# A decoder step on one core: sample rows requested in other places, keys scaled for the state, transposes of two heads in one bank

## The chip, the cores and the metric

The kernel runs on one core of a Trainium2 chip. A core has five engines that each work through a list of their own, in order: TensorE (PE, matmuls and transposes; PEld is its weight load), VectorE (DVE), ScalarE (ACT), GpSimd (POOL) and SyncE (SP, which here only requests transfers; ScalarE requests some too). An instruction waits for semaphores of the others. The metric is the device time of one execution in microseconds.

## The reference

One layer of a decoder, for a prompt of 512 tokens and 8 samples of one token, D = 1024, all in float32:

```python
h = x * (1 + scale) + shift                       # adaLN: silu(c) @ w_ada, six parts
aq, ak, av, mq, mk, mv, mo, mi, mf = split(h @ w_in)
att = moba(aq, ak, av)                            # 8 heads x 64, softmax over blocks of 256 keys
  # samples: 4 pages of 128 keys each from cache_k, cache_v by page_table
C, n, m, hm = mlstm(mq, mk * 128**-0.5, mv, ig, lf)   # 4 heads x 128
  # C_new = g_inter * C + sum_j g_in[j] * v[j] k[j]^T
  # n_new = g_inter * n + sum_j g_in[j] * k[j]
mem = layernorm(hm) * g * sigmoid(mo)
x = layernorm(ALPHA * x + (1 + g1) * ([att, mem] @ w_out))
f = (silu(h2 @ w_gate) * (h2 @ w_up)) @ w_down    # h2: adaLN of x, width 2816
y = layernorm(ALPHA * x + (1 + g2) * f)
```

Outputs are y, the new keys and values, and the states C, n and m, for the prompt and for each sample.

## The kernel before

Each weight block of 128 x 1024 is loaded as float32 (`raw`) and split into two fp32r parts: `whi`, cast by ScalarE (L231), and `wlo` = raw - whi, by VectorE (L232). The activations are split likewise (`hT_hi`, `hT_lo`), and each product is three matmuls (hi x hi, hi x lo, lo x hi), the main matmuls (L391, L644).

The order of all work is written by a small scheduler at build time. A main stream goes through the blocks of w_in, w_out, w_gate, w_up and w_down. After some six main matmuls of 512 columns, or twelve of 256, it calls `tick` (L242): one step of every lane that is due, one weight split, and as many block loads as there are free raw buffers. A lane is a generator for a side job: a query tile of attention, an mLSTM head, a sample's state, the adaLN blocks (`ps_ada`, `ps_s`: rounds of small matmuls over a block). `yield n` in a lane puts its next part n ticks later. A lane that finds no free buffer or PSUM bank asks again in the next tick. So a `yield` moves instructions in the lists of all engines, against the main matmuls and against other lanes. There are eight PSUM banks, 22 large units, 13 halves, 6 rows and 4 squares. Each transfer takes the next of eight semaphores, and a request waits for the transfer that had that semaphore before.

The places that the change touches, in the order of time:

- Start: `cols` (conditioning columns, L285) is requested by ScalarE. `ps_warm` (L330) runs 12 dummy matmuls. `first_h` (L467) transposes the adaLN rows of a chunk (`ps_adat`), makes adaT, hT_hi (ScalarE) and hT_lo (VectorE), and for chunk 0 the first weight split.
- `att_unit(pair, qt)` (L795): for query tile qt and two heads, scores, softmax, then for each head transposes of the probabilities into a bank `ps_pt` and copies into `PT`; one bank a head.
- `sample_attention` (L1229): scores of all samples (`SC`) are transposed into `ps_ss`; own-token scores come from q8 and k8 (`qk`) through `own` and `ps_so`; the exponent `Pm` is read from ps_ss and ps_so; Pm is transposed (`ps_sp`), and `ps_pv` multiplies it with V pages, which `fetch` requests four at a time from SP, with a page number read from a table for each.
- `sample_bc(g)` (L1373): requests rows of k and q for four samples, broadcast over 32 partitions, by ScalarE, eight requests (`kq`). `sample_state(b)` (L1382): a sample's C is loaded, scaled by the forget gate on ScalarE, then on VectorE four state updates (L1393) and four dots (L1396).
- `mlstm_state` (L1155): the prompt's final C and n. Keys are transposed (`ps_mk`), copied (`mk`); values are multiplied by the input gate (`gv`, L1171); `ps_C` sums over tokens. `n_prompt_rows` (L1141) multiplies keys with the gate column.
- `out_fin` (L1699) of the samples: transposes `ps_xs` of the normalised rows.

## Time and profile before

| | |
|---|---|
| median of 3 runs | 795.07 us (792.77 to 795.56) |
| profiled execution | 797.14 us, span 795.4 us |
| mean granted clock of PE | 0.976 |
| PE busy | 756.5 us (95%) |
| PEld, DVE, ACT, POOL busy | 624.6, 408.7, 278.3, 136.7 us |
| chain that ended last | PE 81%, DVE 11%, issue 2%, DMA 2%, ACT 2%, POOL 1% |
| moved | 123.11 MB, mean 155 GB/s |

Times are microseconds from the start of the span. A row of the timeline gives the start, the time that the row's instructions took together (matmuls overlap, so the difference of two starts is what one takes), the engine and the line, and in brackets how long the engine had been idle and what released it. "SPq" and "ACTq" rows are requests of transfers; their time is the time that the engine's list spent on them.

### The profile page before, as it was taken

How to read it: one execution, taken by the hardware profiler on the slowest of the kernel's cores; microseconds unless marked ns; L12 is line 12 of the kernel's file. 1: busy time of each engine (PE TensorE's matmuls, PEld its weight loads, DVE VectorE, ACT ScalarE, POOL GpSimd, SP SyncE). 2: the span in 40 equal slices, each digit the busy share in tenths (PEclk: the TensorE clock that was granted, in tenths of full speed). 3: DMA queues.
4: the chain of work that ended last, by engine and by line, in shares of the span. 5: the costliest groups of instructions: out<-in, count | busy, mean ns of one | idle time of the engine just before them, and what ended most of it. 6: DMA issues, size and time to landing. Idle time of an engine off the chain costs nothing.

```text
span 795.4 us, 14683 instructions
## 1 busy us (share of the span) xinstructions
PE 756.5 (95%) x5790; PEld 624.6 (79%) x5790; DVE 408.7 (51%) x860; ACT 278.3 (35%) x556; POOL 136.7 (17%) x162
## 2 busy tenths in 40 slices
...
GB/s 344 361 215 165 271 209 192 213 203 143 177 206 261 332 207 202 276 71 213 133 137 89 124 109 133 83 103 107 80 80 80 99 87 102 85 80 106 1 42 67
DMA packets 105906, 123.11 MB, mean 155 GB/s; under 512 B 8220, under 2 KB 65696, under 8 KB 105836
## 3 DMA queue, kind: packets, MB, share of 16 engines
...
q10 hardware_dynamic: 8120, 9.23, 3.4%
...
## 4 chain that ended last, share of the span: by engine, by line
PE 81%; DVE 11%; issue 2%; DMA 2%; ACT 2%; POOL 1%; SPq 0%; POOLq 0%; ACTq 0%; DVEq 0%
PE acc L644 35%; PE acc L391 29%; PE ps_ada L405 2%; DVE wlo L232 2%; PE ps_dn L413 1%; PE accl L391 1%; PE ps_num L1061 1%; PE ps_pv L1307 1%; PE ps_sc L802 1%; PE ps_ada L459 1%; PE ps_o L855 1%; PE ps_pt L832 1%; PE ps_ms L1038 1%; DVE st L808 1%; DVE rtmp L1601 1%
## 5 line engine op out<-in xcount | busy, mean ns | idle before, releaser
L232 DVE TENSOR_TENSOR wlo<-raw,whi 128x1024 fp32r<-128x1024 f32 x104 | 138.0, 1334 | 124.5 <-ACT whi L231 117.2
L231 ACT CAST whi<-raw 128x1024 fp32r<-128x1024 f32 x104 | 108.0, 1049 | 154.1 <-PE acc L391 68.7
L644 PE MATMUL acc<-h_hi,whi 128*128 128x256 f32 (+1 forms) x640 | 129.2, 283 | 0.0
L644 PE MATMUL acc<-h_lo,whi 128*128 128x256 f32 (+1 forms) x640 | 128.3, 282 | 0.0
L644 PE MATMUL acc<-h_hi,wlo 128*128 128x256 f32 (+1 forms) x640 | 128.2, 282 | 0.0
L644 PEld LDWEIGHTS acc<-h_hi,whi 128*128 128x128 f32 x640 | 98.9, 188 | 2.6 <-issue 2.5
L644 PEld LDWEIGHTS acc<-h_lo,whi 128*128 128x128 f32 x640 | 99.3, 188 | 0.0
L644 PEld LDWEIGHTS acc<-h_hi,wlo 128*128 128x128 f32 x640 | 98.9, 188 | 0.0
L1216 POOL TENSOR_TENSOR kpage<-kpage,qb 128x512 f32<-128x512 f32 x32 | 42.5, 1352 | 81.2 <-DMA kpage<-in_cache_k_dram 80.8
L391 PE MATMUL acc<-whi,hT_hi 128*128 128x512 f32 x96 | 44.2, 460 | 2.1 <-DVE mv L1007 2.1
L1750 DVE TENSOR_TENSOR vf<-acc,vf 128x256 f32<-128x256 f32 x20 | 8.5, 424 | 72.1 <-PE acc L644 72.1
L391 PE MATMUL acc<-whi,f_hi 128*128 128x512 f32 x112 | 45.4, 405 | 0.0
L391 PE MATMUL acc<-whi,f_lo 128*128 128x512 f32 x112 | 44.2, 395 | 0.0
L391 PE MATMUL acc<-wlo,f_hi 128*128 128x512 f32 x112 | 44.2, 395 | 0.0
L391 PE MATMUL acc<-whi,hT_lo 128*128 128x512 f32 x96 | 39.7, 414 | 0.0
L391 PE MATMUL acc<-wlo,hT_hi 128*128 128x512 f32 x96 | 39.2, 409 | 0.0
L644 PE MATMUL acc<-hT_hi,whi 128*128 128x256 f32 (+1 forms) x160 | 35.9, 304 | 2.9 <-DVE mixA_lo L866 1.5
L1756 POOL COPY fsT<-vf 128x8 f32<-128x8 f32 x20 | 4.8, 239 | 192.5 <-DVE vf L1751 192.5
L397 ACT CAST f_hi<-vf 128x512 fp32r<-128x512 f32 (+1 forms) x24 | 14.0, 585 | 67.9 <-DVE vf L1751 61.9
L1602 POOL TENSOR_TENSOR x<-x,rtmp 128x512 f32<-128x512 f32 x16 | 26.0, 1642 | 65.2 <-DVE rtmp L1601 64.8
L644 PEld LDWEIGHTS acc<-hT_hi,whi 128*128 128x128 f32 x160 | 24.7, 188 | 13.2 <-issue 9.1
L644 PE MATMUL acc<-hT_hi,wlo 128*128 128x256 f32 (+1 forms) x160 | 32.1, 282 | 0.0
...
## 6 DMA issues: line engine op xcount, KB each, us to landing
...
```

Of the source, the lines that this page charges most:

```text
L231: ACOPY(out=t.hi_t, in_=t.raw)
L232: TT(out=t.lo_t, in0=t.raw, in1=t.hi_t, op=ALU.subtract)
L391: mm(ps, lhsT=a, rhs=b, start=start and i == 0, stop=stop and i == n - 1)
L397: ACOPY(out=dst_hi, in_=v)
L405: mm(ps[32 * c:32 * c + 32, 0:P], lhsT=lhs[:, k0 + kk, :], rhs=raw3[:, kk, ts(c, P)], start=start and kk == 0, stop=stop and kk == nk - 1, ...
L413: mm(ps[32 * c:32 * c + 32, 0:256], lhsT=lhs[:, k0 + kk, :], rhs=raw3[:, kk, ts(n, 256)], start=start, stop=stop, tile_position=(0, 32 * c))
L459: mm(ps[32 * c:32 * c + 32, 0:w], lhsT=siluT[:, k, :], rhs=rhs, start=k == 0, stop=k == 7, tile_position=(0, 32 * c))
L644: mm(accs[d, hf][:, 0:hi - lo], lhsT=w, rhs=two(xx, k)[:, lo:hi], start=k == 0 and i == 0, stop=k == 7 and i == 2)
L802: mm(bs[e][:, 0:n], lhsT=two(qT, pair)[eh, ts(qt, P)], rhs=two(kT, pair)[eh, 0:n], start=True, stop=True, tile_position=(64 * e, 0))
L1216: PT_(out=ks[i - 4], in0=ks[i - 4], in1=qb, op=ALU.mult)
L1602: (PT_ if pool_add else TT)(out=dst, in0=dst, in1=tmp, op=ALU.add)
L1750: TT(out=v[:, 0:HALF], in0=a[:, 0:HALF], in1=v[:, 0:HALF], op=ALU.mult)
```

## The change

`cols` is requested by SP. The warm-up has 10 dummies in place of 12; one dummy stands before the first ps_adat and five behind it, and for chunk 0 hT_lo is made ahead of the second half of the split. In att_unit both heads of a pair share a bank for qt 0 and 1, 256 columns each, and both are copied after the second; for qt 2 and 3 the second head comes a tick later. In sample_attention q8, k8 and v8 are requested ahead of the V pages, ps_so comes one tick later, ps_sp two later, ps_pv two ticks behind it, and the memset of its bank is replaced by a first matmul that writes 32 rows of each quadrant. kq is requested two at a time, a tick apart. A sample's dots come a tick after its updates. In mlstm_state the keys are multiplied by the input gate as they leave PSUM (two heads by ScalarE, two by VectorE); values go into ps_C as they are, and the n rows are summed with a column of ones. Two more `yield`s are longer by one (adaLN, ps_xs).

```diff
@@ -40,3 +40,3 @@
 N_HALVES = 13
-N_WARM = 12
+N_WARM = 10
 FF_GROUPS = ((0, 6), (6, 14), (14, 22))
@@ -284,3 +284,3 @@
     cols = cst.tile([P, 200], F32, name="cols")
-    dma_a(out=cols, in_=columns)
+    dma(out=cols, in_=columns)
     cT = cols[:, 0:72].rearrange("p (k r) -> p k r", r=9)
@@ -327,6 +327,10 @@
     ACT(out=siluT[:, :, 0:9], in_=cT, func=AF.Silu)
-    busy = banks.get("ps_warm")
-    for _ in range(N_WARM):
-        mm(busy[:, 0:P], lhsT=ident, rhs=ident, start=True, stop=True)
-    banks.put(busy)
+
+    def keep_busy(n):
+        busy = banks.get("ps_busy")
+        for _ in range(n):
+            mm(busy[:, 0:P], lhsT=ident, rhs=ident, start=True, stop=True)
+        banks.put(busy)
+
+    keep_busy(N_WARM)
     adaT = cst.tile([P, 6, 8, 9], F32, name="adaT")
@@ -366,2 +370,4 @@
     ones = ones.to_broadcast([4, T])
+    one1 = cst.tile([P, 1], F32, name="one1")
+    nc.gpsimd.memset(one1, 1.0)
     mhalf = cst.tile([P, 4], F32, name="mhalf")
@@ -468,2 +474,4 @@
         k0, nk = chunks[i]
+        if i == 0:
+            keep_busy(1)
         ps = banks.get("ps_adat")
@@ -481,2 +489,4 @@
         squares.put(sb)
+        if i == 0:
+            keep_busy(5)
         for s in range(2):
@@ -490,2 +500,7 @@
         xT = first["xT", i]
+        hT = get("hT", [nk, T])
+        for j in range(nk):
+            k = k0 + j
+            TS(out=hT[:, j, :], in0=xT[:, j, :], scalar1=adaT[:, 1, k, 8:9], scalar2=adaT[:, 0, k, 8:9],
+               op0=ALU.mult, op1=ALU.add)
         if i == 0:
@@ -496,11 +511,8 @@
                 bias=adaT[:, 0, k, 8:9])
-        if i == 0:
-            first_split(0, 1)
-        hT = get("hT", [nk, T])
         for j in range(nk):
-            k, kk = k0 + j, (k0 + j) % 2
-            TS(out=hT[:, j, :], in0=xT[:, j, :], scalar1=adaT[:, 1, k, 8:9], scalar2=adaT[:, 0, k, 8:9],
-               op0=ALU.mult, op1=ALU.add)
+            kk = (k0 + j) % 2
             TT(out=hT_lo[kp][:, kk, 0:T], in0=hT[:, j, :], in1=hT_hi[kp][:, kk, 0:T], op=ALU.subtract)
         put(xT, hT)
+        if i == 0:
+            first_split(0, 1)
         TT(out=hsT[:, ks, 0:8], in0=xsT[:, ks, :], in1=adaT[:, 1, ks, 0:8], op=ALU.mult)
@@ -581,3 +593,3 @@
                 return
-            yield 1
+            yield 2
             pt = yield from lane_bank("ps_adat")
@@ -828,4 +840,7 @@
                 yield 1
-            PT = pts[h]
-            ps = yield from lane_bank("ps_pt")
+            if e == 0 or qt >= 2:
+                if e:
+                    yield 1
+                bank = yield from lane_bank("ps_pt")
+            ps = bank[:, 256 * e:256 * e + 256] if qt < 2 else bank
             for kt in range(qt + 1):
@@ -833,10 +848,8 @@
             rows.put(pr)
-            for k0 in range(0, qt + 1, 2):
-                kn = min(2, qt + 1 - k0)
-                src = ps[:, k0 * P:(k0 + kn) * P].rearrange("p (k q) -> p k q", q=P)
-                w = T if k0 == 0 else 256
-                o = qt * P if k0 == 0 else (qt - 2) * P
-                dst = PT[:, k0 * T:k0 * T + 2 * w].rearrange("p (k q) -> p k q", q=w)[:, 0:kn, o:o + P]
-                (VCOPY if qt % 2 else ACOPY)(out=dst, in_=src)
-            banks.put(ps)
+            if qt < 2 and e == 0:
+                continue
+            todo = ((h - 1, bank[:, 0:256]), (h, ps)) if qt < 2 else ((h, ps),)
+            for h_, ps in todo:
+                pt_copy(qt, pts[h_], ps)
+            banks.put(bank)
         att_done[pair] += 1
@@ -845,2 +858,11 @@
 
+    def pt_copy(qt, PT, ps):
+        for k0 in range(0, qt + 1, 2):
+            kn = min(2, qt + 1 - k0)
+            src = ps[:, k0 * P:(k0 + kn) * P].rearrange("p (k q) -> p k q", q=P)
+            w = T if k0 == 0 else 256
+            o = qt * P if k0 == 0 else (qt - 2) * P
+            dst = PT[:, k0 * T:k0 * T + 2 * w].rearrange("p (k q) -> p k q", q=w)[:, 0:kn, o:o + P]
+            (VCOPY if qt % 2 else ACOPY)(out=dst, in_=src)
+
     def att_pv(pair):
@@ -1144,3 +1166,3 @@
             for h in range(HM):
-                mm(psn[32 * h:32 * h + 1, 0:P], lhsT=gin[:, t, h:h + 1], rhs=two(mk, t)[:, ts(h, P)],
+                mm(psn[32 * h:32 * h + 1, 0:P], lhsT=one1, rhs=two(mk, t)[:, ts(h, P)],
                    start=t == 0, stop=t == NT - 1, tile_position=(0, 32 * h))
@@ -1162,13 +1184,12 @@
                 nc.tensor.transpose(ps[:, ts(h, P)], two(mkT, h)[:, ts(t, P)], ident)
-            ACOPY(out=two(mk, t), in_=ps)
+            for h in range(HM):
+                d, s = two(mk, t)[:, ts(h, P)], ps[:, ts(h, P)]
+                if h % 2:
+                    TS(out=d, in0=s, scalar1=gin[:, t, h:h + 1], scalar2=None, op0=ALU.mult)
+                else:
+                    nc.scalar.mul(out=d, in_=s, mul=gin[:, t, h:h + 1])
             banks.put(ps)
-            yield 1
+            yield 2
         put(mkT)
         for h in range(HM):
-            gvs = []
-            for t in range(NT):
-                gv = wk.tile([P, P], F32, name="gv", tag="gv", bufs=4)
-                nc.scalar.mul(out=gv, in_=mv1[t // 2][:, t % 2, h, 0:P], mul=gin[:, t, h:h + 1])
-                gvs.append(gv)
-            yield 2
             if h == 3:
@@ -1177,3 +1198,4 @@
             for t in range(NT):
-                mm(psC[:, 0:P], lhsT=gvs[t], rhs=two(mk, t)[:, ts(h, P)], start=t == 0, stop=t == NT - 1)
+                mm(psC[:, 0:P], lhsT=mv1[t // 2][:, t % 2, h, 0:P], rhs=two(mk, t)[:, ts(h, P)],
+                   start=t == 0, stop=t == NT - 1)
             sb = yield from slot(squares, "Csb")
@@ -1236,2 +1258,12 @@
             yield 1
+        qk = yield from slot(halves, "qk8", n=2)
+        q8, k8 = qk[0][0:NB, :], qk[1][0:NB, :]
+        vo = yield from slot(units, "vo", [832], spare=2)
+        v8 = vo[0:NB, 0:512]
+        PTo = vo[0:NB, 512:576].rearrange("p (b r) -> p b r", r=8)
+        PTs = vo[:, 576:832].rearrange("p (j b r) -> p j b r", j=4, r=8)
+        PTw = vo[:, 576:832]
+        dma(out=q8, in_=r_scr[0])
+        dma(out=c4(k8), in_=s_tok(1))
+        dma(out=c4(v8), in_=s_tok(2))
         vu = yield from slot(units, "vpage", [2, 512], n=2)
@@ -1248,11 +1280,2 @@
         fetch(1)
-        qk = yield from slot(halves, "qk8", n=2)
-        q8, k8 = qk[0][0:NB, :], qk[1][0:NB, :]
-        vo = yield from slot(units, "vo", [832])
-        v8 = vo[0:NB, 0:512]
-        PTo = vo[0:NB, 512:576].rearrange("p (b r) -> p b r", r=8)
-        PTs = vo[:, 576:832].rearrange("p (j b r) -> p j b r", j=4, r=8)
-        dma(out=q8, in_=r_scr[0])
-        dma(out=c4(k8), in_=s_tok(1))
-        dma(out=c4(v8), in_=s_tok(2))
         ps = yield from lane_bank("ps_ss")
@@ -1271,3 +1294,3 @@
         TT(out=own, in0=own, in1=negoff[:, :, None].to_broadcast([NB, NB, 8]), op=ALU.add)
-        yield 1
+        yield 2
         pso = yield from lane_bank("ps_so")
@@ -1288,3 +1311,3 @@
         TS(out=Pm, in0=Pm, scalar1=st[:, 6:7], scalar2=None, op0=ALU.mult)
-        yield 1
+        yield 3
         ps = yield from lane_bank("ps_sp")
@@ -1298,5 +1321,5 @@
         banks.put(ps)
+        yield 2
         for g in range(2):
             bank = yield from lane_bank("ps_pv")
-            nc.vector.memset(bank, 0.0)
             for j in range(4):
@@ -1306,4 +1329,10 @@
                 for c in range(4):
-                    mm(bank[32 * c:32 * c + 8, :], lhsT=PTs[:, j, 4 * g + c, :], rhs=sets[i % 2][c],
-                       start=j == 0, stop=False, tile_position=(0, 32 * c))
+                    if j == 0:
+
+                        o = 8 * (4 * g + c)
+                        mm(bank[32 * c:32 * c + 32, :], lhsT=PTw[:, o:o + 32], rhs=sets[i % 2][c],
+                           start=True, stop=False, tile_position=(0, 32 * c))
+                    else:
+                        mm(bank[32 * c:32 * c + 8, :], lhsT=PTs[:, j, 4 * g + c, :], rhs=sets[i % 2][c],
+                           start=False, stop=False, tile_position=(0, 32 * c))
                 if i < 6:
@@ -1376,5 +1405,7 @@
         for i, tl in ((2, kb), (1, qb)):
-            for h in range(HM):
-                dma_a(out=tl[32 * h:32 * h + 32], in_=at(r_scr, (i * NB + 4 * g) * 512 + h * P,
-                                                         [[0, 32], [512, 4], [1, P]]))
+            for h0 in range(0, HM, 2):
+                for h in (h0, h0 + 1):
+                    dma_a(out=tl[32 * h:32 * h + 32], in_=at(r_scr, (i * NB + 4 * g) * 512 + h * P,
+                                                             [[0, 32], [512, 4], [1, P]]))
+                yield 1
         sm["kq", g] = kb, qb
@@ -1394,2 +1425,3 @@
                 op0=ALU.mult, op1=ALU.add)
+        yield 1
         for j in range(4):
@@ -1715,3 +1747,3 @@
                 TS(out=xs, in0=xs, scalar1=s[:, 12:13], scalar2=s[:, 14:15], op0=ALU.subtract, op1=ALU.mult)
-                yield 1
+                yield 2
                 pb = yield from lane_bank("ps_xs2")
```

Three places of the lists. First SP, where the samples' attention starts; `qk` and `vo` are q8, k8 and v8. Before:

```order
L186 DMA raw<-in_w_in_dram 128x2x512
L1197 TENSOR_LOAD pt_i
L1197 ISA x2
L1198 ISA
L1198 DMA vpage<-in_cache_v_dram 128x512
...
L1255 DMA qk_2841<-r_scr 8x512
L1256 DMA qk_2842<-s_scr 8x4x128
L1257 DMA vo<-s_scr 8x4x128
L1126 DMA negM<-m_scr 128x512
L186 DMA raw<-in_w_ada_dram 128x2x512
L1414 DMA m_2914<-in_state_n_dram 8x512
```

And changed:

```order
L186 DMA raw<-in_w_in_dram 128x2x512
L1148 DMA negM<-m_scr 128x512
L186 DMA raw<-in_w_ada_dram 128x2x512
L1266 DMA qk_2692<-r_scr 8x512
L1267 DMA qk_2693<-s_scr 8x4x128
L1268 DMA vo<-s_scr 8x4x128
L1219 TENSOR_LOAD pt_i
L1219 ISA x2
L1220 ISA
L1220 DMA vpage<-in_cache_v_dram 128x512
...
L1446 DMA m_2914<-in_state_n_dram 8x512
```

The five requests have moved from behind the eight pages to ahead of them; the samples' n state (`m_2914`) is still behind them.

Second ScalarE, from the gate matrix E to the exponent Pm. Before:

```order
L1027 ACTIVATE E<-negM,gcol 128x384
L1378 DMA kq<-r_scr 32x4x128 x8
L1027 ACTIVATE E<-negM,gcol 128x256
L1282 ACTIVATE Pm,sst<-ps_ss,sst 64x512
L1283 ACTIVATE Pm,sst<-ps_so,sst 64x8
```

And changed:

```order
L1408 DMA kq<-r_scr 32x4x128 x2
L1049 ACTIVATE E<-negM,gcol 128x256
L1408 DMA kq<-r_scr 32x4x128 x2
L1049 ACTIVATE E<-negM,gcol 128x128
L231 CAST whi<-raw 128x1024
L1453 ACTIVATE m_2914<-m_2914,o_1807 8x128 x4
L1408 DMA kq<-r_scr 32x4x128 x2
L783 ACTIVATE s_sb<-ps_s_2619 128x128
L785 DMA s_scr<-s_sb 128x128
L1305 ACTIVATE Pm,sst<-ps_ss,sst 64x512
L1306 ACTIVATE Pm,sst<-ps_so,sst 64x8
```

Pm stood behind the eight requests; it now stands behind six, a weight cast and the scaling of the n state.

Third VectorE, around the product of the samples' mLSTM output with its gate (h by mo, whose transposes are `ps_h`, copied to mixsT). Before:

```order
L232 TENSOR_TENSOR wlo<-raw,whi 128x1024
L1039 TENSOR_TENSOR AT<-ps_ms,E 128x384
L1509 TENSOR_TENSOR h_3989<-h_3989,mo_3749 8x512
L1084 TENSOR_TENSOR s<-s 128x4
L1087 SCALAR_TENSOR_TENSOR hm<-hm,s,gs_3896 128x128 x2
```

And changed:

```order
L1633 TENSOR_TENSOR rtmp<-acc,G 128x512
L1634 TENSOR_TENSOR x_4039<-x_4039,rtmp 128x512
L1691 BN_STATS ls<-x_4039 128x6
L1692 BN_AGGR ls<-ls 128x2
L1160 TENSOR_SCALAR ls<-ls 128x1
L1694 TENSOR_SCALAR x_4039<-x_4039,ls 128x1024
L232 TENSOR_TENSOR wlo<-raw,whi 128x1024
L1541 TENSOR_TENSOR h_4314<-h_4314,mo_3679 8x512
```

It stood before the second last mLSTM head's scaling; it now stands behind a residual tile with its LayerNorm.

## Rows read from the trace of the kernel before

**Rows 1.** Stretches: length, busy us by engine, granted clock, DMA share, GB/s.

```profile
102.00:105.40 3.40, 3.40 (x10) 2.62 (x9) 1.05 (x4) 0.00 (x0) 2.48 (x2) 0.50 0.55 211
...
218.00:221.50 3.50, 3.50 (x10) 2.77 (x9) 0.17 (x2) 0.61 (x1) 1.70 (x4) 0.51 0.82 276
...
228.30:235.20 6.90, 5.12 (x33) 2.81 (x34) 3.64 (x13) 1.10 (x3) 0.00 (x0) 0.51 0.72 207
...
262.50:265.90 3.40, 3.40 (x12) 0.93 (x11) 2.06 (x11) 0.00 (x0) 0.00 (x0) 0.50 1.03 364
...
337.60:344.40 6.80, 4.67 (x17) 4.26 (x18) 1.90 (x6) 4.41 (x12) 0.02 (x1) 0.50 0.19 36
```

**Rows 2.** Timeline: start, us, engine, line, out<-in, idle before and releaser.

```profile
9.61 0.60 PE L391 MATMUL acc<-hT_hi,whi 128*128 128x512 f32 x1 [1.19 <-ACT hT_hi L495]
...
11.55 0.79 PE L391 MATMUL acc<-hT_lo,whi 128*128 128x512 f32 x1 [1.34 <-DVE hT_lo L504]
...
21.89 1.05 ACT L521 CAST whi<-wq 128x1024 fp32r<-128x1024 f32 x1 [1.37 <-DMA wq<-in_w_in_dram]
```

**Rows 3.** Timeline, VectorE and PE at the second transposes.

```profile
100.96 0.41 DVE L840 COPY PT<-ps_pt 128x256 f32<-128x256 f32 x1
...
101.43 0.44 PE L832 MATMUL ps_pt<-ident,pr 128*128 128x128 f32 x2 [2.02 <-DVE PT L840]
```

**Rows 4.** Timeline, SP's requests and PE, 203 to 218 us.

```profile
203.13 9.23 SPq L1198 DMA_DIRECT2D vpage<-in_cache_v_dram  x8
...
212.46 0.34 SPq L1255 DMA_DIRECT2D qk<-r_scr  x1
...
217.49 0.17 PE L1274 MATMUL ps_so<-ident,own 8*64 8x8 f32 x1 [3.85 <-DVE own L1271]
```

**Rows 5.** Timeline, ScalarE's requests and PE, 218 to 233 us.

```profile
218.79 4.97 ACTq L1378 DMA_DIRECT2D kq<-r_scr  x8
...
228.64 0.66 PE L1292 MATMUL ps_sp<-ident,Pm 64*128 64x64 f32 x4 [4.28 <-DVE Pm L1288]
...
230.84 1.89 PE L1307 MATMUL ps_pv<-vpage,vo 128*8 128x512 f32 x8 [1.44 <-DVE ps_pv L1301]
```

**Rows 6.** Timeline, VectorE and PE, 253 to 262 us.

```profile
253.64 1.13 DVE L1393 SCALAR_TENSOR_TENSOR C<-kq,gvs,C 128x128 f32<-128x128 f32 x4
...
261.17 0.50 PE L391 MATMUL acc<-whi,hT_hi 128*128 128x512 f32 x1 [2.11 <-DVE mv L1007]
```

**Rows 7.** Timeline, ScalarE and PE, 330 to 342 us.

```profile
330.37 0.59 ACT L1163 COPY mk<-ps_mk 128x512 f32<-128x512 f32 x1 [0.77 <-PE ps_mk L1162]
...
339.29 1.26 ACT L1171 ACTIVATE gv<-mv,gin 128x128 f32<-128x128 f32 x4
...
339.73 2.08 PE L1178 MATMUL ps_C<-mk,gv 128*128 128x128 f32 x8 [4.60 <-ACT gv L1171]
```

**Rows 8.** Timeline, PE at 386 us.

```profile
386.71 0.66 PE L1719 MATMUL ps_xs<-ident,xs 8*128 8x8 f32 x8 [1.04 <-DVE xs L1715]
```

**Rows 9.** Timeline, VectorE: a tile's first residual row, the split behind.

```profile
351.29 0.67 DVE L1601 TENSOR_TENSOR rtmp<-acc,G 128x512 f32<-128x512 f32 x1
...
355.24 1.22 DVE L232 TENSOR_TENSOR wlo<-raw,whi 128x1024 fp32r<-128x1024 f32 x1
```

**Rows 10.** Stretches, two of VectorE's.

```profile
321.50:341.60 20.10, 15.14 (x90) 13.08 (x89) 10.52 (x34) 14.22 (x31) 1.02 (x1) 0.90 0.87 273
...
344.90:361.00 16.10, 16.10 (x164) 10.74 (x164) 14.33 (x23) 6.53 (x15) 1.10 (x2) 1.00 0.42 137
```

**Rows 11.** Timeline, PE: a round of small matmuls, then main ones.

```profile
352.22 0.64 PE L405 MATMUL ps_ada<-raw,siluT 128*32 128x128 f32 x16
...
352.79 0.50 PE L391 MATMUL acc<-whi,mixA_hi 128*128 128x512 f32 x1
...
353.13 0.40 PE L391 MATMUL acc<-wlo,mixA_hi 128*128 128x512 f32 x1
...
353.36 0.39 PE L391 MATMUL acc<-whi,mixA_lo 128*128 128x512 f32 x1
```

6 lines of the change are left out of this document (3 added, 3 removed).

## Prediction

> **What bounds the kernel now.** I read the page's busy table first: PE is busy 756.5 of 795.4 us, so only idle PE time or slow PE time is to be had. Then the PE timeline, to list each gap in front of a matmul with its releaser, and the table of stretches, to see the granted clock behind each gap. The reader is to see two things. Thirteen gaps of over half a microsecond lie between 8 and 395 us; the nine that the change touches stand in rows 2 to 8. From 395 us on the order of the instructions is unchanged. And after each gap of 2 us or more follows a stretch of 3.4 to 6.9 us with a granted clock near 0.50, which is 1.2 GHz instead of 2.4 [rows 1]. A matmul then takes about twice the time, so a stretch costs about half its PE busy time: 1.7, 1.75, 2.55, 1.7 and 2.35 us in the five rows. Then, for each gap, the timeline of the engine that released it: what stood in front of the releasing instruction in that engine's own order. Each engine works its list strictly in order, so that is where the change acts. The sum is made against the profiled execution, 797.14 us, which is 2.1 us above the median of the three timed runs, 795.07.
>
> **Start.** The first hT_hi and hT_lo release PE after 1.19 and 1.34 us [rows 2]. The change asks for cols earlier, takes two matmuls off the warm-up, puts six into PE's waits around the first adaT transposes, and makes hT_lo ahead of the weight split on VectorE. But the second weight block is released by its own landing at 21.89 us, with ScalarE waiting for it [rows 2]: behind that point the start is paced by transfers, and what is won ahead of it is largely waited away. I take 1.0 us; bounds -0.5 (the dummies stand in front of real matmuls) and 2.5 (both gaps). Cover of the dummies: PE waits there anyway.
>
> **Transposes of two heads in a bank (qt below 2).** PE's second pair of transposes waited 2.02 us for VectorE's copy of the first pair, which sat behind reductions [rows 3]. With both in one bank nothing lies between them. Worth 2.02 + 1.7 of clock, less 0.6: ps_o now follows the second head's two copies, which come one behind the other (0.41 each). 3.1 us; bounds 0 and 3.7.
>
> **Sample rows ahead of the V pages.** ps_so waited 3.85 us; its input was asked for behind eight V pages whose requests held SP for 9.23 us [rows 4]. The three loads now go first, so they are asked about 9 us earlier and ps_so one tick later. The gap goes: 3.85 + 1.75 = 5.6 us. Bounds 2 and 5.6.
>
> **kq two a step, memset away, longer yields.** ps_sp waited 4.28 us because ScalarE's exponent Pm stood behind eight kq requests of 4.97 us; ps_pv waited another 1.44 us for a memset [rows 5]. The memset has gone, since the first matmul of each group now writes all 32 rows (same 512 columns, so nothing on PE), and three more ticks stand ahead of ps_sp. 4.28 + 1.44 + 2.55 = 8.3 us, less what is late next. In the new ScalarE list Pm stands behind m x4, and that needs the n state, which SP asks for behind the V pages. On PE the next user of the bank of ps_ss is the first 128x512 ps_ms, which waits for Pm. Count from ps_ss: four SP requests (1.5 us, 212.46 to 213.98 in the old list; the row shows the first) and the pages (9.23) put the n request near +10.5; a wait of the w_ada load for its buffer, 1.0; landing, 2.0 (estimate); m x4, 1.26 as four like multiplications in [rows 7]; two kq requests at 4.97/8, 1.24; the copy and store of s, 0.6; Pm itself, 0.7: +17.3. PE gets there after 48 main matmuls at 0.23, four 16-matmul rounds at 0.57 [rows 11] and about 0.9 of small ones, +14.2. So 3.1 us stay, and 1.7 of clock: 8.3 - 4.8 = 3.5 us. Bounds -1 and 8.3.
>
> **A step between a sample's two groups.** The mv copy that frees PE's bank stood behind three samples' state updates and dots; 2.11 us of PE [rows 6]. In the new VectorE list one group of four (1.13) remains ahead of it: 2.11 + 1.7 - 1.1 = 2.7 us. Bounds 0 and 3.8.
>
> **Keys scaled in place of values.** The 16 gv multiplications on ScalarE go, four of them took 1.26 us and the last stood behind the hm scaling; ps_C waited 4.60 us for it [rows 7]. The four 128x512 copies of mk (0.59 each) become 16 evictions of 128x128, half of them on each engine, at 0.32 by the gv row. ps_hm of the last head needed the same hm chain, so the gap would fall on it, but it now has 48 main matmuls (11 us) between the last ps_num and itself, against 18 before. 4.60 + 2.35 - 0.5 = 6.4 us; bounds 2 and 6.9. A bank of ps_mk is emptied by both engines in turn: the new lists make each eviction wait for the other engine's. That is 4 x 0.32 = 1.3 in place of 0.59 us a bank, 2.8 us over four banks; I put 1.0 on the path, bounds 0 and 2.8, since VectorE is nearly full there (below).
> The Trainium skill ("PSUM — Partial Sum Buffer", section "PSUM bank collisions raise a hardware error") says that two engines may not touch the same bank and quadrant at once, reads included, so the turns can't be dropped. No row of before has both engines on one bank; without the rule the term would be 0.
>
> **ps_xs one tick later.** 1.04 us [rows 8]; a tick is six main matmuls, 1.4 us. I take 0.9.
>
> **What is late next at the samples' end.** The samples' mLSTM ends some 14 ticks later than before, for its steps now yield more. Its output gate product h8 stood ahead of the last heads' scaling; in the new VectorE list it stands behind the third residual eviction, that tile's LayerNorm and a weight split. Such a chain took from 351.29 to 355.24, 3.95 us, and the split 1.22 [rows 9], h8 itself about 0.7: 5.8 us from the end of the third accumulation. On PE only six main matmuls and two rounds lie between, 2.5 us. Stall 3.3 us if VectorE keeps up. It does not quite: in the old stretch 344.9 to 361 it was busy 14.33 of 16.1 us [rows 10], and the samples' ps_nu copy, statistics and the n rows add about 3 us, so I add 1.3: 4.6 us. Behind ps_h the next ps_os waits for the copy of ps_h, which stands behind the fourth tile's LayerNorm: 3.95 - 1.4 - 0.3 = 2.3 us. With 1.7 of clock: 8.6 us; bounds 0 and 13. ScalarE's waits for the samples' C loads, now requested closer to their use: 1.0, bounds 0 and 20 (last rival).
>
> **Sum.** 1.0 + 3.1 + 5.6 + 3.5 + 2.7 + 6.4 + 0.9 = 23.2 us won; 8.6 + 1.0 + 1.0 = 10.6 us lost. Net 12.6: 797.1 - 12.6 = 784.5 profiled, and with the same 2.1 us between profile and median 782.5 us.
>
> **Rivals.** (A) No stall at the samples' end, VectorE having worked ahead: 782.5 - 8.6 = 773.9 us. For it: before 341 us VectorE was busy only 10.52 of 20.1 us [rows 10]. Against: three state groups and three dot groups (1.13 each) and 8 evictions (2.6) now fall there too, 19.9 of 20.1 us. Chance 0.15.
> (B) ScalarE stays blocked near 205 to 235 us: the gaps only move from ps_so and ps_sp to ps_ms. The old loss of 13.9 us (5.6 + 8.3) then stays in place of 4.8: 782.5 + 9.1 = 791.6 us, just within half a per cent of before. For it: the n request still lies behind the V pages. Chance 0.12.
> (C) The gaps shrink but the clock still falls at the remaining ones of 1 to 2 us. Three of the five stretches (about 1.7 + 1.7 + 2.3) come back: 788.2 us. For it: a gap of 2.02 us was enough [rows 1, 3]. Against: where nothing is waited for, as in 344.9 to 361, the clock is 1.00 [rows 10]. Chance 0.12.
> The Trainium skill ("TensorE: Matmul & The Clock Gate", "Part 1: The HAM clock gate") says that one kernel showed different numbers of slow matmuls from run to run, and that a model shouldn't be fitted to a count of them. By it each remaining gap could cost its stretch in one execution and not in another, and the sum would come out at about 785.9 us if two more such stretches of 1.7 fell in; one profile can't show that.
> (D) Slower. The last three samples' C loads are requested a few entries ahead of the scaling by the forget gate on ScalarE. If each holds ScalarE, VectorE's state group behind it waits, and with it the AT products, mk evictions and mixM_lo that PE needs, in a stretch where VectorE has 0.2 us to spare. At the length for which the kq requests held ScalarE, 4.97 us [rows 5], and 1.7 of clock each, three cost 20 us: 802.5 us. It decides from about 2.5 us each, where the net gain has gone (3 x (2.5 + 1.7) = 12.6). Chance 0.06.
>
> **How the numbers follow.** Forecast 0.55, at 782.5 us, own spread about 777 to 788. Range 772 to 792: it takes in A, C and most of B, and leaves out D and the tails. What a measurement can tell from no change here is about 0.5%, 4 us: faster means below 791.1. Faster: nearly all of the forecast, A, most of C, under half of B, 0.81; same 0.13; slower 0.06.
>
> **What would show it.** Right: ps_so, ps_sp, ps_pv, the second ps_pt and the third ps_C have no wait over 0.6 us; a wait of 2 to 5 us stands at the first 128x512 ps_ms, released by ScalarE's Pm; one of 3 to 6 us at the samples' last ps_h, released by VectorE's gate product, and one of 2 us at the ps_os behind it. Wrong: ps_h without a wait (A), a wait of over 8 us at ps_ms (B), granted clock near 0.5 behind gaps of under 2 us (C), ScalarE waiting for C loads between 290 and 345 us (D), or a span unchanged behind 40 us while the start alone moves.

## The result: slower by 0.7%

The changed kernel took 800.87 us (median of 20 executions, 792.61 to 804.29), the kernel before 795.52 us beside it: a ratio of 1.0066, 95% interval 1.0049 to 1.0084. One execution of the kernel before took 1213.06 us, the other 19 between 792.70 and 798.11; it does not bear on the median. The forecast was 782.5 us, faster by 12.6. So 17.9 us stand between forecast and result (12.6 and the 5.3 lost). The profiled execution took 803.13 us, with a span of 801.4 us. The page's busy table of it:

```profile
PE 759.4 (95%) x5798; PEld 625.3 (78%) x5798; DVE 411.2 (51%) x866; ACT 273.7 (34%) x544; POOL 136.4 (17%) x163
```

PE's busy time hardly differs from before (756.5). To see where the time went I lined up the main matmuls of the two traces, the k-th of one with the k-th of the other. By the times of the kernel before, the changed kernel is level until 97 us, ahead by 4.2 at 126, 5.0 at 206, 9 to 10 at 220, 20.7 at 276; it falls back to 4.4 at 325, wins 5 again by 347, is level at 359, and behind by about 6 from 411 us to the end. The prediction's sum of the steps up to 276 us was 15.9 (1.0 + 3.1 + 5.6 + 3.5 + 2.7). The lead there is larger, since part of it is side work put off (the lead of e11, below, falls from 18.1 at this matmul to 12.7 at 363 us); 26.6 us were lost between 276 and 411.

PE's timeline after the change, its longer waits (in brackets the wait and what ended it):

```profile
9.70 0.50 PE L397 MATMUL acc<-hT_hi,whi 128*128 128x512 f32 x1 [0.25 <-ACT hT_hi L510]
...
127.77 0.46 PE L814 MATMUL ps_sc<-kT,qT 64*128 64x128 f32 x2 [1.76 <-DVE st L828]
...
211.51 0.19 PE L1297 MATMUL ps_so<-ident,own 8*64 8x8 f32 x1
...
216.98 1.13 PE L1060 MATMUL ps_ms<-mqT,mkT 128*128 128x512 f32 x2 [0.93 <-ACT s_sb L783]
...
226.42 0.80 PE L1060 MATMUL ps_ms<-mqT,mkT 128*128 128x128 f32 x2 [1.85 <-DVE AT L1061]
...
300.42 0.50 PE L397 MATMUL acc<-whi,mixA_hi 128*128 128x512 f32 x1 [2.20 <-DVE mk L1188]
...
313.84 0.63 PE L1184 MATMUL ps_mk<-ident,mkT 128*128 128x128 f32 x4 [4.18 <-DVE s L1092]
...
350.01 0.56 PE L1545 MATMUL ps_h<-ident,h 8*128 8x8 f32 x4 [7.42 <-DVE h L1541]
...
353.99 1.08 PE L419 MATMUL ps_os<-raw,mixsT 128*32 128x256 f32 x8 [0.56 <-DVE mixsT L1547]
...
393.81 0.58 PE L397 MATMUL acc<-h_hi,wlo 128*128 128x256 f32 x1 [2.57 <-DVE wlo L232]
...
409.01 0.39 PE L397 MATMUL acc<-h_hi,whi 128*128 128x264 f32 x1 [1.30 <-ACT h_hi L403]
```

The waits of [rows 2 to 7] went or shrank as forecast: 1.19 to 0.25 at the start, 3.85 at ps_so gone, 4.28 at ps_sp and 1.44 at ps_pv gone, 2.02 at ps_pt, 2.11 behind mv and 4.60 at ps_C gone. In their place stand waits that total more: 2.20, 4.18, 7.42, 2.57, 1.30. The table of stretches at the half clock, 1.2 GHz (length, busy us by engine, granted clock, DMA share, GB/s), answers [rows 1]:

```profile
226.22:229.64 3.42, 3.22 (x22) 2.30 (x23) 1.08 (x7) 0.92 (x2) 0.46 (x1) 0.50 0.77 232
301.32:304.73 3.41, 3.41 (x15) 3.02 (x14) 3.31 (x13) 1.54 (x3) 0.00 (x0) 0.50 0.34 29
314.97:318.38 3.41, 3.41 (x9) 2.65 (x8) 2.98 (x8) 0.96 (x4) 0.00 (x0) 0.50 1.06 404
345.69:359.34 13.65, 8.77 (x41) 5.41 (x42) 8.14 (x15) 1.04 (x1) 1.10 (x2) 0.50 0.57 192
393.48:396.89 3.41, 3.08 (x14) 3.08 (x15) 2.62 (x6) 0.00 (x0) 0.57 (x2) 0.50 0.54 158
```

With one more of 3.41 us at 24.84 they sum to 30.7 us, and so did those of before; but they now lie behind the new waits, 13.65 us of them around ps_h. There the PE was busy 8.77 us at half clock, which costs about 4.4 us on top of 7.42 + 0.56: 12.4 us in all, where the prediction had 8.6.

What held ps_h is VectorE's order. Its timeline from the third tile's residual rows (rtmp, x) to the gate product (h<-h,mo):

```profile
342.06 0.67 DVE L1633 TENSOR_TENSOR rtmp<-acc,G 128x512 f32<-128x512 f32 x1
...
347.33 0.81 DVE L1694 TENSOR_SCALAR x<-x,ls 128x1024 f32<-128x1024 f32 x1 [0.66 <-POOL ls L1161]
348.05 1.22 DVE L232 TENSOR_TENSOR wlo<-raw,whi 128x1024 fp32r<-128x1024 f32 x1
349.19 0.67 DVE L1541 TENSOR_TENSOR h<-h,mo 8x512 f32<-8x512 f32 x1
...
353.75 0.18 DVE L1547 COPY mixsT<-ps_h 128x32 f32<-128x32 f32 x1
```

And ScalarE's, with the product's input, and two loads that it waited for:

```profile
296.54 0.33 ACTq L1416 DMA_DIRECT2D C<-in_state_C_dram  x1
...
312.52 0.72 ACT L1421 ACTIVATE C<-C,fi 128x512 f32<-128x512 f32 x1 [6.68 <-DMA C<-in_state_C_dram]
...
340.43 1.65 ACT L1538 ACTIVATE h<-h,s 8x128 f32<-8x128 f32 x4 [1.54 <-DVE s L1535]
...
357.97 1.04 ACT L231 CAST whi<-raw 128x1024 fp32r<-128x1024 f32 x1 [13.32 <-DMA raw<-in_w_out_dram]
```

The product's input was ready at 342.08; the product ran at 349.19, behind the LayerNorm and the weight split, as the prediction said. A consequence that it did not have: the split (wlo) frees the raw buffers, so SP's requests of weights wait for the same late engine. The table of what SP waited for between 330 and 362 us (total, times, longest):

```profile
SPq L186 <- DVE wlo L232: 21.2, 5, 8.2
```

ScalarE then stood 13.32 us without a weight block, and PE was busy 12.02 of the 20 us from 340 to 360, at a mean granted clock of 0.66. Two stretches answer [rows 10]. In the first the prediction had worked out 19.9 us of VectorE in 20.1; it was busy 15.35. So VectorE was late by the order of its list and by what it waited for, and not because it was full.

```profile
321.50:341.60 20.10, 18.33 (x148) 13.40 (x147) 15.35 (x38) 10.53 (x21) 1.50 (x2) 1.00 0.39 117
...
340.00:360.00 20.00, 12.02 (x74) 7.36 (x67) 14.32 (x25) 4.83 (x8) 1.10 (x2) 0.66 0.55 188
```

### The profile page after: what moved, and what is told of

Its sections match the earlier page's. It is cut to its first block, busy times and chain, and to the rows that moved or that the text cites. A ratio compares the mean times of both kernels' runs of the same rounds, so it can differ in the third digit from the quotient of the medians.

```text
span 801.4 us, 14700 instructions
## 1 busy us (share of the span) xinstructions
PE 759.4 (95%) x5798; PEld 625.3 (78%) x5798; DVE 411.2 (51%) x866; ACT 273.7 (34%) x544; POOL 136.4 (17%) x163
## 4 chain that ended last, share of the span: by engine, by line
PE 71%; DVE 10%; DMA 7%; ACT 6%; issue 3%; SPq 1%; POOL 1%; ACTq 0%; POOLq 0%; DVEq 0%
PE acc L656 35%; PE acc L397 23%; DMA C<-in_state_C_dram 2%; DVE wlo L232 2%; PE ps_ada L411 2%; ACT v L1705 1%; PE ps_dn L419 1%; ACT whi L231 1%; PE accl L397 1%; DMA wq<-in_w_in_dram 1%; PE ps_sc L814 1%; DVE rtmp L1633 1%; PE ps_pt L847 1%; DMA x<-in_x_prompt_dram 1%; PE ps_o L877 1%
## 5 line engine op out<-in xcount | busy, mean ns | idle before, releaser
L656 PE MATMUL acc<-hT_lo,whi 128*128 128x256 f32 (+1 forms) x160 | 32.3, 283 | 0.0
```

The costliest lines, as they stand in the source:

```text
L656: mm(accs[d, hf][:, 0:hi - lo], lhsT=w, rhs=two(xx, k)[:, lo:hi], start=k == 0 and i == 0, stop=k == 7 and i == 2)
```

## The experiments

The edits are to the changed kernel or to e6, as said. A ratio is to the kernel before. The rivals at first: the waits at the samples' end come from the samples being late (the split requests of kq and the tick before the dots make them so); from the state lane running beside the samples; from C loads behind bulk loads; or from single steps elsewhere that are worth less than forecast.

**e1: the eight kq requests at once.**

```diff
-                yield 1
         sm["kq", g] = kb, qb
```

> The changed kernel (median 800.9 us) with one part undone: the eight kq requests of a group stand together again. Theory F (the end is too full: the samples' states, later by the added steps, fall onto 290 to 355 us, where VectorE also has the last two mLSTM heads and the residual, and PE waits for VectorE): the samples' last ps_h comes 54 main matmuls earlier in the order (954 in place of 1008), so its 7.4 us wait and the 13.6 us of half clock behind it go, and about 4 us of the old Pm wait come back near 220 us: 789 to 795 us. Theory K (ScalarE and VectorE take turns on a bank of ps_mk, and that holds both): the turns stay, so 800 to 806 us. Theory C (the samples' C loads wait behind the loads of x, b_ada and G, 4.2 us of PE at 310 us): the C loads come earlier, 796 to 800 us.

788.68 us, 0.9916 (0.9889 to 0.9944): 12.2 us better than the changed kernel, from one line, and just below F's 789 to 795. No wait at ps_h is left. PE's timeline shows the old cost back, and more, near 219 us:

```profile
219.57 2.08 PE L1060 MATMUL ps_ms<-mqT,mkT 128*128 128x512 f32 x2 [5.55 <-ACT s_sb L783]
```

ScalarE's timeline shows why: the requests hold it, longer than the 4.97 us of [rows 5].

```profile
207.02 7.52 ACTq L1408 DMA_DIRECT2D kq<-r_scr  x7
```

So the pairs do remove a wait there, and are still worth minus 12 us.

**e3: values scaled, as before** (the whole of mlstm_state and n_prompt_rows).

> The changed kernel with the prompt's final state as it was before: values scaled on ScalarE, mk copied whole, n rows with the gate column. Theory F: the samples stay late (ps_h at main matmul 1008 as before this undo), VectorE loses 16 small evictions' half (about 2.8 us), so the 7.4 us wait shrinks only by some 2 us: 797 to 803 us. Theory K: the waits at 298 us (2.2 us, released by mk) and at ps_C go, and with them the lateness that the 7.4 us wait shows: 788 to 793 us. Theory C: the 4.2 us at 310 us stay: 798 to 802 us.

798.13 us, 1.0024 (0.9997 to 1.0052): 2.7 us below the changed kernel, but the two intervals still touch. ps_h waits 5.71 us. Scaled keys bring nothing that can be seen beside the late samples.

**e4: ps_h three ticks later.**

```diff
         TT(out=h8, in0=h8, in1=o_s, op=ALU.mult)
-        yield 1
+        yield 4
```

> The changed kernel with the samples' last ps_h three steps later in PE's order (after 1026 main matmuls in place of 1008), nothing else moved by hand. Theory F: the wait of 7.4 us at ps_h is PE arriving too early; about 5 us of main matmuls go in front of it, and the half clock behind it gets shorter: 793 to 797 us. Theory K and theory C: what is late comes from further ahead, the gap only moves to the next instruction that needs VectorE or a weight block: 799 to 802 us.

798.93 us, 1.0031 (1.0012 to 1.0049). The wait at ps_h went, but 3.52 us came back at a main matmul behind VectorE's wlo and 3.52 at ps_os. The 793 to 797 expected by F, the forecast's own mechanism at ps_h, were missed: VectorE's list is late there as a whole, and PE meets it at the next thing that it needs.

**e5: pairs for the first four samples only, dots at once.**

```diff
-                yield 1
+                if g == 0:
+                    yield 1
...
                 op0=ALU.mult, op1=ALU.add)
-        yield 1
```

> The changed kernel with kq asked two a step only for the first four samples, and a sample's dots right behind its updates again. Theory F: the samples end earlier (ps_nu after 948 main matmuls in place of 978, ps_h after 984 in place of 1008), all else is in the same place: the 7.4 us wait shrinks to 0 to 3 us, the last C load is asked for earlier and its wait falls too: 788 to 794 us. Theory K: 798 to 802 us. Theory C: the 4.2 us at 310 us go, the rest stays: 794 to 797 us.

797.38 us, 1.0032 (1.0016 to 1.0049), where F had 788 to 794. ps_h waited 4.50, and a main matmul 4.80 behind mk. A little less late is not enough. The place behind a residual tile is not the only one that costs, either. In e5 the gate product stands ahead of the first residual row (342.39), but behind a split that waits for ScalarE's cast. VectorE's timeline:

```profile
334.96 1.23 DVE L232 TENSOR_TENSOR wlo<-raw,whi 128x1024 fp32r<-128x1024 f32 x1 [2.71 <-ACT whi L231]
336.10 0.67 DVE L1541 TENSOR_TENSOR h<-h,mo 8x512 f32<-8x512 f32 x1
```

**e6: e1 with ps_xs one tick earlier, as before.**

```diff
-                yield 2
+                yield 1
                 pb = yield from lane_bank("ps_xs2")
```

> The kernel of the first experiment (eight kq requests together, 788.7 us) with the samples' xs transposes one step after their rows again, as before the change. Theory X (the added step puts the product vs behind a whole residual tile with its LayerNorm on VectorE, 3.95 us; ScalarE's list behind it, h_hi and the weight casts, is late by as much, PE waits 1.5 and 2.0 us at 377 and 392 us, and 7 us of half clock follow): the 1.0 us gap at ps_xs comes back and some 5 us go, 783 to 786 us. Rival (those waits come from the end being full, as the waits before them): 787 to 790 us.

786.31 us, 0.9888 (0.9867 to 0.9910): 2.4 us better than e1, with intervals that overlap, and just above the 783 to 786 expected. The traced execution, 783.14 us, is the fastest of its six. **e7: that step alone, the pairs kept.**

> The changed kernel (800.9 us) with that one step undone alone. Theory X: 795 to 798 us, the waits at 391 us (2.6, wlo) and 408 us (1.3, h_hi) gone. Rival (VectorE is late there because of the samples' lateness): 799 to 802 us, those waits stay.

796.44 us, 1.0004 (0.9984 to 1.0024): 4.4 us better than the changed kernel. The tick had been priced at +0.9, for the 1.04 us wait that it removes. VectorE's order shows what it makes late. In e1, with the extra tick, the samples' product vs stands behind a whole residual tile (its timeline):

```profile
378.91 0.68 DVE L1632 TENSOR_TENSOR rtmp<-acc,G 128x512 f32<-128x512 f32 x1
...
382.14 1.15 DVE L1693 TENSOR_SCALAR x<-x,ls 128x1024 f32<-128x1024 f32 x1 [0.66 <-POOL ls L1161]
383.20 0.20 DVE L1752 TENSOR_TENSOR vs<-ps_xs,a 128x64 f32<-128x64 f32 x1
```

In e6 it stands ahead of it:

```profile
376.12 0.22 DVE L1752 TENSOR_TENSOR vs<-ps_xs,a 128x64 f32<-128x64 f32 x1
...
377.28 0.68 DVE L1632 TENSOR_TENSOR rtmp<-acc,G 128x512 f32<-128x512 f32 x1
```

The cast of vs on ScalarE and the h_hi that the next block needs follow it. The waits of 2.57 and 1.30 us in the changed kernel are its price there, and e7 has neither; but in e7 PE waits 2.66 us at ps_xs and 3.41 us at half clock stay. Between the 1080th and the 1230th main matmul the changed kernel loses 5.5 us on the kernel before, e7 2.1.

**e8: the state lane waits until all samples are done.**

```diff
-        while sum(ms_done) < NT * HM:
+        while sum(ms_done) < NT * HM or sm_done[0] < NB:
```

> The changed kernel with the prompt's final state (ps_mk to ps_C) begun only when the samples' eight states are done (first ps_mk after 966 main matmuls in place of 918); nothing taken out. Theory F, in the form that the prompt's state and last heads lie on the same stretch as the samples' states: the waits between 298 and 328 us (2.2, 4.2, 1.0) shrink to under 3 us in sum, the 7.4 us at ps_h stay or shrink a little, 793 to 798 us. Rival C (the last C load is late by itself, behind the bulk loads): the 4.2 us stay, 799 to 803 us.

804.67 us, 1.0093 (1.0061 to 1.0126; four executions), ps_h 8.89 us. Both ranges on record (793 to 798 and 799 to 803) were missed. Sharing VectorE with the state lane is not shown to be the cause: apart, the kernel is no better.

**e9: e6 with q8, k8 and v8 requested behind the V pages, as before.**

> The kernel of the first run of this set with q8, k8 and v8 requested behind the eight V pages again. If the rows ahead of the pages are worth what was forecast, ps_so waits again for 2 to 4 us, with half clock behind it, and the total is 3 to 6 us over that run: 787 to 791 us. If the later stall at the first 128x512 ps_ms (5.6 us, behind the kq requests) takes it over, the two are within 1.5 us: 783 to 787 us.

785.22 us, 0.9872 (0.9849 to 0.9894; four executions), no worse than e6. The old ps_so wait returns, and the one at ps_ms shrinks from 4.19 to 1.75. PE's timeline of e9:

```profile
214.37 0.17 PE L1297 MATMUL ps_so<-ident,own 8*64 8x8 f32 x1 [3.99 <-DVE own L1294]
...
222.14 1.13 PE L1060 MATMUL ps_ms<-mqT,mkT 128*128 128x512 f32 x2 [1.75 <-ACT s_sb L783]
```

and of e6, where ps_so doesn't wait:

```profile
218.12 2.08 PE L1060 MATMUL ps_ms<-mqT,mkT 128*128 128x512 f32 x2 [4.19 <-ACT s_sb L783]
```

The two waits of e9 make 5.74 us; e1, e11 and e14, which have e6's order here, wait 5.38 to 5.66 at ps_ms alone. With the requests at once the early rows only choose where PE waits. In the changed kernel, with the pairs, this was not tried.

**e10: the changed kernel with the bulk loads of x, gates and LayerNorm rows six ticks later.**

```diff
-    spawn(ln1_rows())
-    spawn(gate_rows(0, 2048, "1"))
-    spawn(ln_rows(ln1_g, ln1_b, ALPHA), 2)
+    spawn(ln1_rows(), 6)
+    spawn(gate_rows(0, 2048, "1"), 6)
+    spawn(ln_rows(ln1_g, ln1_b, ALPHA), 8)
```

> The changed kernel (800.9 us) with the loads of x, b_ada, G and the LayerNorm vectors asked for six steps later. Theory C (the last C load, asked for at 296.5 us, waits behind these 4 MB, holds ScalarE for 6.7 us and PE for 4.2): that wait goes; G's two buffers are also taken later, so the samples' C loads come earlier and ps_h stands after 984 main matmuls in place of 1008: 792 to 797 us. Theory F (VectorE's work in 290 to 350 us is too much, whatever is loaded when): the 4.2 us go, 5 us or more stay at ps_h or ahead of it: 797 to 800 us.

806.19 us, 1.0140 (1.0117 to 1.0164), above both ranges on record. The C load's 6.68 us on ScalarE and PE's 4.18 are gone, which fits the bulk loads as what held that load for 16 us. But the whole is slower, with 10.05 at ps_h. The gate product now stands ahead of all residual rows, and VectorE waits for ScalarE, which has the late loads and the stores of the state in front of the product's input:

```profile
344.99 0.68 DVE L1541 TENSOR_TENSOR h<-h,mo 8x512 f32<-8x512 f32 x1 [6.42 <-ACT h L1538]
```

So e10 put another late step in front of ps_h, and what the late C load costs by itself is not shown.

**e11: e6 with the dots at once.** (The `yield 1` in front of the dots taken out, as in e5.)

> The best kernel so far (kq together, xs step undone, 786.3 us) with a sample's four dots right behind its updates, as before the change. The forecast gave the added step 2.7 us (the wait for the mv copy of 2.1 us and the half clock behind it). If that holds: 788 to 790 us, with a wait of 1 to 2 us released by mv. If the step only makes the samples later, 784 to 787 us.

784.13 us, 0.9859 (0.9835 to 0.9883), the best of all. No wait behind mv came back; a 0.81 us one behind Z stands at 256 us. The intervals of e6 and e11 overlap, so the dots' tick costs 0 to 2 us; its forecast gain of 2.7 is not there.

**e14: e6 with values scaled, as before; e15: e11 with values scaled.**

> The best kernel so far (786.3 us) with the prompt's final state as before the change: values scaled on ScalarE, mk copied whole. The forecast gave the scaled keys 6.4 us less 1.0 for the turns. If that holds: a wait of 3 to 5 us at ps_C or ps_hm, released by gv, and 790 to 793 us. If the turns cost what the missing gv saves: 785 to 788 us, the waits of 1.1, 0.5, 2.1 and 0.6 us at ps_hm and ps_C gone.

> The kernel with kq together, the xs step undone, a sample's dots at once and the values scaled as before: what is left of the change is the start, the shared bank, the rows ahead of the pages, the longer yields there and the missing memset. From the two single runs (784.1 for the dots, 785.0 for the values, against 786.3): 782 to 785 us, if the two add up 782.8.

784.96 us, 0.9876 (0.9855 to 0.9896), and 784.97 us, 0.9877 (0.9848 to 0.9905): scaled keys are worth nothing, where 5.4 was forecast. PE's timeline of e14 has the old wait on gv:

```profile
320.33 1.35 PE L1200 MATMUL ps_C<-mk,gv 128*128 128x128 f32 x8 [1.02 <-ACT gv L1193]
...
326.14 2.08 PE L1200 MATMUL ps_C<-mk,gv 128*128 128x128 f32 x8 [4.45 <-ACT gv L1193]
```

and that of e6 the waits that took its place, where the engines empty a bank of ps_mk in turn:

```profile
316.40 0.66 PE L1131 MATMUL ps_hm<-ident,hm 128*128 128x128 f32 x4 [1.08 <-DVE mk L1188]
318.46 0.94 PE L1199 MATMUL ps_C<-mk,mv 128*128 128x128 f32 x6 [0.53 <-DVE mixM_lo L1137]
...
321.50 1.16 PE L1199 MATMUL ps_C<-mk,mv 128*128 128x128 f32 x8 [2.10 <-ACT mk L1190]
...
323.28 0.54 PE L1199 MATMUL ps_C<-mk,mv 128*128 128x128 f32 x2 [0.62 <-DVE mk L1188]
```

5.47 us went and 4.33 came (sums of these rows).

**e12: e6 with a bank for each head's transposes, as before.**

> The best kernel so far (786.3 us) with a bank for each head's transposes and no added step, as before the change. The forecast gave the shared bank 3.1 us. If that holds: the wait of some 2 us at the second ps_pt near 98 us comes back with half clock behind it, 788 to 791 us. If another wait takes it over: 785 to 787 us.

793.75 us, 0.9980 (0.9963 to 0.9996). The edit also takes out the tick of the second head for qt 2 and 3; bank and tick together are worth 7.4 us, more than twice the forecast of 3.1 and above the 788 to 791 expected. PE's timeline shows the old wait, and one that grew from 4.19 in e6:

```profile
100.91 0.69 PE L844 MATMUL ps_pt<-ident,pr 128*128 128x128 f32 x2 [2.05 <-DVE PT L852]
...
227.61 2.07 PE L1050 MATMUL ps_ms<-mqT,mkT 128*128 128x512 f32 x2 [6.63 <-ACT Pm L1295]
```

and a stretch behind the first of them is back at half clock:

```profile
100.83:104.24 3.41, 3.33 (x9) 2.75 (x10) 1.17 (x5) 0.00 (x0) 1.22 (x1) 0.50 0.74 264
```

2.05 + 1.7 are the forecast's own terms. At ps_ms PE waits 2.44 longer than in e6, which was not foreseen; the half clock there lasts 6.83 us for 3.41, but PE is busy 2.93 of them against 3.06, so it costs no more. That makes 6.2. The late step is ScalarE's Pm behind the eight requests again, which stand at 220.32 here and at 205.76 in e6. The rest of the 7.4 is not found, nor which of bank and tick moves the requests.

**e16 and e18: e6, requests at once, with the samples' mLSTM 4 and 8 ticks later.** These ask how much of the pairs' cost is lateness alone; the edit shown is that of e18.

```diff
         for b in range(NB):
+            if b == 0:
+                yield 8
             if b % 4 == 0:
```

> The kernel with kq together and the xs step undone (786.3 us), with the samples' mLSTM begun four steps later and nothing else. The kq requests stay eight in a row. Theory P (place): four steps suffice for the last two prompt heads and the final state to get their buffers ahead of the last samples (ps_mk after 918 main matmuls in place of 966, ps_h after 984 in place of 954), so VectorE has the residual in front of the gate product and PE waits at ps_h: 793 to 799 us. Theory Q (it is the split requests themselves, ScalarE's list with them between other work): 785 to 789 us.

> As the run with the samples four steps late (788.5 us), but eight, which is the lateness that the split requests of both groups bring. The kq requests stay together. If lateness alone explains the changed kernel with its xs step undone (796.4 us): 793 to 798 us, the gate product now behind the fourth residual tile, a wait of 4 to 9 us at ps_h. If the split requests cost something of their own: 787 to 791 us.

Four ticks: 788.51 us, 0.9927 (0.9901 to 0.9953); of the two ranges on record 793 to 799 (lateness by itself is the price) was missed and 785 to 789 met. Eight: 794.38 us, 0.9985 (0.9971 to 0.9998), 8.1 us more than e6, so at eight lateness is the price after all. What the lists show as different is the place of the gate product on VectorE. In e16 it is still ahead of the residual tiles:

```profile
331.78 0.67 DVE L1542 TENSOR_TENSOR h<-h,mo 8x512 f32<-8x512 f32 x1
...
334.60 0.69 DVE L1634 TENSOR_TENSOR rtmp<-acc,G 128x512 f32<-128x512 f32 x1 [0.99 <-PE acc L397]
```

In e18 it is behind the fourth tile's LayerNorm and a split:

```profile
349.70 0.81 DVE L1695 TENSOR_SCALAR x<-x,ls 128x1024 f32<-128x1024 f32 x1 [0.67 <-POOL ls L1161]
350.43 1.22 DVE L232 TENSOR_TENSOR wlo<-raw,whi 128x1024 fp32r<-128x1024 f32 x1
351.56 0.67 DVE L1542 TENSOR_TENSOR h<-h,mo 8x512 f32<-8x512 f32 x1
```

and PE waits 10.70 us at ps_h, against 1.24 in e16 and nothing in e6. e7, with the pairs, stands only 2 us above e18, and their intervals overlap; whether the requests cost anything of their own is not shown.

**e17: e7 with pairs for the last four samples only** (as in e5's first edit, with `g == 1`).

> The changed kernel with the xs step undone and kq two a step only for the last four samples. The final state comes late again (ps_mk from 960), but the samples' ps_h stands after 984 main matmuls. Theory P, with ps_h behind the residual as what costs: a wait of 3 to 8 us at ps_h, 791 to 797 us. If it is the early final state that costs: 785 to 789 us.

786.74 us, 0.9905 (0.9877 to 0.9933); ps_h waits 3.48. The 791 to 797 expected from ps_h's place were missed, and the 785 to 789 of the other theory, that an early final state costs, were met. That theory alone fails too: e16 has the early state and is cheap, e8 has it late and is dear. Pairs for the last four samples cost nearly nothing, all of them 10 us. In e5, with pairs for the first four, the kernel stays 13.2 us above e11, of which the step at ps_xs explains 2.4 to 4.4; so it seems to matter which samples are late, and not only by how many ticks.

**e19: e7 with the gate product on GpSimd.**

```diff
-        TT(out=h8, in0=h8, in1=o_s, op=ALU.mult)
+        PT_(out=h8, in0=h8, in1=o_s, op=ALU.mult)
```

> The changed kernel with the xs step undone (796.4 us), and the samples' gate product (8x512) on GpSimd in place of VectorE; the order of all else stays. If the 7.4 us at ps_h are the product's place in VectorE's list: ps_h waits under 2 us, the ps_os behind it waits 1 to 5 us for VectorE's copy of ps_h, which stays behind the fourth tile, and the total is 790 to 794 us. If VectorE is late as a whole and PE waits for whatever comes next: 795 to 798 us.

799.34 us, 1.0042 (1.0019 to 1.0065): no better than e7, and ps_h still waits 6.00 us in the traced execution (795.44 us). The expectation (under 2 us there, 790 to 794) failed for a plain reason, and the other range, 795 to 798, was passed by a little. GpSimd's timeline:

```profile
342.46 0.55 POOL L1161 TENSOR_TENSOR ls<-ls,mhalf 128x1 f32<-128x1 f32 x1 [10.21 <-DVE ls L1160]
342.97 1.25 POOL L1541 TENSOR_TENSOR h<-h,mo 8x512 f32<-8x512 f32 x1
```

The product's input was ready at 337.8, but GpSimd's own list holds the LayerNorm's step of the same tile ahead of it, and waited 10.21 us for that. The tile was passed on one engine and met on the other.

## Why the prediction was wrong

The wait that it named for the loss is the one that PE has in the changed kernel: at ps_h, for the gate product behind a residual tile and a split. Two steps of the sum failed. The first is the balance of the added ticks: what they win (3.5, 2.7 and 0.9) against "What is late next at the samples' end" (8.6) and the C loads (1.0), a net loss of 2.5. By medians, undoing three ticks (kq pairs, ps_xs, dots) takes the changed kernel from 800.9 to 784.1 (e11): they cost 16.7 us. (The 3.5 also holds the removed memset and the ticks at ps_sp and ps_pv, which e11 keeps.) The second is that the gains of the sample rows (5.6) and the scaled keys (6.4 - 1.0) were added to the others in full; undone in e6, neither is worth anything. All that e11 keeps is worth 11.4 us, forecast 15.1. The differences, 14.2 and 3.7, are the 17.9.

Lined up, the 996th main matmul of the changed kernel starts 0.7 us behind that of e11; 12.2 us more arise up to the 1032nd, around ps_h and ps_os, and 5.4 between the 1080th and the 1230th, behind the step at ps_xs. So the waits of 2.20 and 4.18 us ahead of ps_h, which e11 doesn't have, are no net loss against it by then.

Of the prediction's signs, 2 to 5 us at the first ps_ms were 0.93, 3 to 6 at ps_h were 7.42, and 2 at the ps_os behind it 0.56; D's sign, ScalarE waiting for a C load, was seen once (6.68). Point by point:

- **ps_xs one tick later**: +0.9 forecast, -4.4 (e7) and -2.4 (e6 against e1) measured. The step priced the wait that the tick removes and not the instruction that it puts behind a residual tile. The rows for that price were at hand ([rows 9]).
- **A step between a sample's two groups**: +2.7 forecast, 0 to -2 measured (e11, e15). The wait behind mv went, but without the tick it does not come back in the new order either.
- **kq two a step, with what is late next**: 3.5 - 8.6 - 1.0 = -6.1 forecast, -10.1 (e6 against e7) to -12.2 (e1) measured. Lateness alone costs 8.1 at eight ticks (e18), so the 8.6 was near. Its place had more (12.4 in the trace): VectorE's delay also held the weight requests. The pairs do win something near ps_ms: 0.93 + 1.85 and 1.6 of clock are left in the changed kernel, 4.4, nearly the 4.8 forecast. Without the pairs PE loses 5.7 there in e6 and 7.4 to 7.8 in e1, e11 and e14 (wait and half of the busy time at half clock). That is 1.3 to 3.4 won, where the prediction set its stall against the old order's 8.3. The C load that ScalarE waits for was forecast at 1.0. It was 4.18 + 1.7 at one place: the mechanism of rival D, once instead of three times. What it adds to the whole is not shown (e10).
- **Keys scaled**: 6.4 - 1.0 forecast, 0 measured (e14, e15); the 2.7 that the changed kernel gains without them (e3) is within the noise. The wait on gv did go. The turns between the engines took its place: I had put 1.0 of at most 2.8 on the path; the waits in e6 are 4.33.
- **Sample rows ahead of the V pages**: 5.6 forecast, nothing measured (e9, with the requests at once). The wait only moved to ps_ms. Rival B described this move ("the gaps only move from ps_so and ps_sp to ps_ms"); it holds for ps_so in e9.
- **Transposes of two heads in a bank**: 3.1 forecast. Lined up with the kernel before, the lead grows by just that at this place, from 0.4 at the 290th main matmul to 3.5 at the 312th. On e6 the bank and the tick of qt 2 and 3 are worth 7.4 together (e12), part of it at ps_ms.
- **Start**: 1.0 forecast. The traces are within 0.4 us of each other up to 97 us; the other traces with this start are ahead by 0.1 to 1.9 at the 290th main matmul, so the 1.0 is not refuted.

What is left of the 11.4 after 7.4 for the bank belongs to the removed memset and the ticks around ps_sp and ps_pv, which weren't tried alone.

What is shown is that these ticks cost the time: taken out, it comes back (e1, e7, e11), and late samples without pairs bring back 8.1 of the pairs' 10.1 (e18). That the cost jumps where the gate product falls behind a residual tile is argued. The lists of e16 and e18 fit it; in e5 and e10 the product stands ahead of all residual rows, and PE still waits 4.50 and 10.05 us at ps_h.

Rival C was half right. The clock fell behind 1.85 us at 226, but not behind 1.76 us at 127. At that place the traces differ: behind 1.77 us in e11 it stayed at 1.00, behind 1.69 us in e15 it was 0.50 for 3.41 us. The Trainium skill ("TensorE: Matmul & The Clock Gate", "Part 1: The HAM clock gate") warns against fitting a model to counts of slow matmuls from one run. The times agree in so far as 2 of the 20 executions of the changed kernel took 793 us and the others 799 to 804; the two had a mean granted clock of 0.986 and 0.987, the others 0.973 to 0.982, but which stretches were missing in them, no trace shows. The rule of the Trainium skill ("PSUM — Partial Sum Buffer", section "PSUM bank collisions raise a hardware error") that two engines may not touch one bank and quadrant at once agrees with the order seen: in e6 VectorE stands idle 0.43 to 0.44 us until ScalarE is through with its part of a ps_mk bank. Each waits for the other's semaphore, so no run shows what would happen without the turns.

Open: which step makes e5 dear and e17 cheap, whether the split requests cost anything beyond lateness (e18 and e7), and why the changed kernel's executions spread over 12 us.
